# Last projection's first operands made product by product and tied behind the fold copies; second norm's modulation sums moved ahead of the output products

## The chip, the cores and the metric

One core of a Trainium2 chip runs the whole program. The metric is device time in microseconds (us), the median over several executions. The trace quoted here is of one further execution that was profiled.

## The reference, cut to what matters

Two layers of a hybrid backbone over 1024 tokens of 1024 features, in float32, batch 1. The even layer has a convolution branch and a recurrent branch behind one input projection, each with a gate, and one output projection. The odd layer pools, gates and projects again.

```python
shift, scale, gate = split(silu(c) @ mod_w[l] + mod_b[l], 3)   # modulation, per layer
hx = rmsnorm(x, norm_g[l]) * (1 + scale) + shift
# even layer (l = 0)
va, vg, ga, xb, gb = split(hx @ ev_w_in, 5)
y_a = conformer_conv(va, vg) * silu(ga)
y_b = rglru(xb) * silu(gb)
x = x + gate * (concat(y_a, y_b) @ ev_w_out)
# odd layer (l = 1)
u, g = split(hx @ od_w_in, 2)
d = multiscale_pool(u)                       # linear along the tokens
y = einsum("bngi,gij->bngj", d, w_grp) * od_scale
x = x + gate * ((y * silu(g)) @ od_w_out)
return rmsnorm(x, final_g)
```

The kernel uses that pooling is linear: it multiplies the group matrix w_grp into the input weights of u first (the *folds*), and pools after that.

## The kernel before, in words

**Products.** Features lie on the 128 partitions, tokens along the free axis, cut into two halves of 512. Every float32 operand is split into a high part (a cast on ACT, line 98) and a low part (source minus high on DVE or POOL, line 99), and each 128x512 product is three matmuls: high by high, high by low, low by high. Large projections run as `quad`: a 2x2 blocked product done with seven block products in place of eight, on PSUM tiles `qa_`, `qc_` and `qb_`. Its right-hand operands are named b11, t1, t2, b21, t3, b22, t4 in the order in which the products use them, each with parts `h` and `l`. The seven left-hand operands (`wq_..._1` to `wq_..._7`) are made of two raw weight tiles by `wquad_steps`: sums on DVE (lines 1120 to 1129), casts on ACT, low parts on DVE. The first three products are number 1 (into `qa`), number 5 (into `qc`) and, after `qa` has been copied to `qb` on ACT (line 1156), number 6 (into `qb`). A result leaves PSUM by `put`; for the first output projection this is `x <- qc, m, x` on DVE (line 1445), that is x plus gate times product.

**Order.** The code is written in one order for all engines; a scheduler then places each engine's instructions by readiness and priority, and evictions (`tc.high_priority(offset=EVAC)`) carry a higher priority. `tc.issue_after(i)` makes what stands under it wait in this order until instruction `i` has been placed, on whatever engine.

**Stages around the change** (times of the profiled execution).

- Up to about 666 us: the last products of the convolution gate (`ga`), each multiplied into the branch `u` on DVE (line 1402), from which the operands `ya_b11` to `ya_t4` of the output projection are made.
- 666 to 749 us: the first output projection `woa`, four quads for output rows (0,1), (2,3), (4,5), (6,7). The updated stream x1 is squared and summed on the way (`n1acc`).
- Modulation of the second norm: `mod_halves` is a generator of 16 steps, eight for each half of the features. At the start of a half it loads that half of c into the one tile `cH` (line 248) and applies Silu on ACT (line 249). Each step loads two 128x512 tiles of the transposed modulation weights (`mod`, line 1357, out of a ring of four scratch tiles `t` that others use too), and DVE multiplies each by c and sums along the row (line 1358); in the second half tiny operations (128x1) finish the shift `m1` and the scale `a1` (lines 1361 and 244).

```python
for _ in range((4, 3, 0, 0)[i]): next(mods)        # gate loop, i = 0..3
for _ in range((4, 5, 0, 0)[m // 2]): next(mods)   # inside the output quad of rows m, m+1
```

- 749 to 795 us: the folds of groups 2 and 3. `fold_in` loads the group matrix (`graw`, line 258) and splits it to `gh` and `gl`; `w_raw` loads a tile of u's weights (`wr_wu`, line 1468) and splits it to `wh_wu` and `wl_wu`, the low part on POOL. Each product `fold` is copied out by ACT (`fo <- fold`, line 275) and stored by a DMA on ACT's queue (line 276), since the last projection loads its weights from there. Between them the second norm's root: row sums on PE, `rt_n <- ms_n` on ACT (line 1519), reciprocal and split on DVE (`hl_n`, line 1523), and `rs` on PE, which spreads it over the partitions. Then `scaled` (DVE, line 1563) multiplies x1 by norm and scale, in place.
- From 795 us: the last layer's input projection, quads `_v` (pooled part) and `_g` (gate) in turn. Its operands are `x_b11` and so on, split by `split_x` with the shift added (ACT line 1557, DVE line 1558).

```python
wv0 = v_weights(0, ring_first)
for i in range(KH):                      # KH = 4
    b11, b21 = x1[i][:, HALF[0]], scaled(0, KH + i)
    split_x("b21", i, b21, shift(KH + i), None)
    b12, b22 = scaled(1, i), scaled(1, KH + i)
    t = block_sums(b11, b12, b21, b22, ttile(f"xt3_{i}"), nc.vector)
    split_x("t1", i, t["t1"], None, nc.vector)
    ...                                  # then t2, t3, b22, t4 of the same i
```

Of the kernel before, what the change touches and what calls it, by code (L numbers as in the profile page):

```python
# [1 line left out]

# [1 line left out]

# [17 lines left out]
H = 512  # L22
HALF = (slice(0, H), slice(H, S))
# [28 lines left out]
def body(ctx, tc, xT, ctxT, cc, ccol, modT, modW, win, gw, wout, wu, grp, wg, wo1, small, edge, ident, outT):  # L52
# [24 lines left out]
    def ttile(name):  # L77
        return tpool.tile([P, H], F32, tag="t", name=name)
# [18 lines left out]
    def split(src, hi, lo, eng):  # L97
        return (nc.scalar.copy(hi, src),  # L98
                eng.tensor_tensor(out=lo, in0=src, in1=hi.bitcast(F32), op=sub))
# [149 lines left out]
        nc.scalar.activation(t, t, AF.Silu)  # L249


    graws = {}

    def fold_in(g, g_tile, raw_tile):
        gh, gl = [], []
# [9 lines left out]
    def fold_steps(g, kp, gs, w, out_tile):  # L265
        (gh, gl), (wh, wl) = gs, w
        for s in range(2):
            ps = psum(f"fold_{g}_{kp}_{s}")
            for i in range(4):
                kc = slice(i * 2 * P + s * P, i * 2 * P + (s + 1) * P)  # L270
                yield ps, wh[:, kc], gh[i], i == 0, False
                yield ps, wh[:, kc], gl[i], False, False
                yield ps, wl[:, kc], gh[i], False, i == 3
            o = out_tile(f"fo_{g}_{kp}_{s}")
            nc.scalar.copy(o, ps)
# [807 lines left out]
        return split(src, hi[i], lo[i], nc.vector)  # L1083


    def block_sums(b11, b12, b21, b22, t3, eng):
        eng.tensor_tensor(out=t3, in0=b22, in1=b12, op=sub)
        eng.tensor_tensor(out=b12, in0=b12, in1=b11, op=sub)
        eng.tensor_tensor(out=b11, in0=b22, in1=b12, op=sub)
        eng.tensor_tensor(out=b21, in0=b21, in1=b11, op=sub)  # L1090
        return dict(t2=b11, t1=b12, t3=t3, t4=b21, b22=b22)

    loaded, parted = [None], []


    def wquad(*args):
        ops = {}
        for _ in wquad_steps(ops, *args):
            pass
        return tuple(ops[n] for n in range(1, 8))  # L1100

    def wquad_steps(ops, src, name, ring, late=False):
        raw = []
        for i in range(2):
            r = wpool.tile([P, D], F32, tag="wr", name=f"wr_{name}_{i}")
            loaded[0] = nc.sync.dma_start(r, src[i])
            raw.append(r)
        a11, a12 = [raw[0][:, h] for h in HALF]
        a21, a22 = [raw[1][:, h] for h in HALF]

        def op(v, i):
            t = ring(f"wq_{name}_{i}")
            parted[:] = split(v, t[:, HALF[0]], t[:, HALF[1]], nc.vector)
            return t

        ops[1] = op(a11, 1)
        if late:
            ops[4] = op(a22, 4)
        s3 = ttile(f"ws_{name}")
        nc.vector.tensor_tensor(out=s3, in0=a11, in1=a21, op=sub)  # L1120
        nc.vector.tensor_tensor(out=a21, in0=a21, in1=a22, op=add)
        nc.vector.tensor_tensor(out=a11, in0=a21, in1=a11, op=sub)
        if not late:
            ops[5] = op(a21, 5)
            yield
        ops[6] = op(a11, 6)
# [261 lines left out]
    for i in range(KH):  # L1388
        (b11, b12), (b21, b22) = [[us[j][:, h] for h in HALF] for j in (i, KH + i)]
        t1, t2, t3, t4 = b11, ttile(f"yat2_{i}"), b12, b21  # L1390
        for j in (i, KH + i):
            if i:
                w = wload(win[2 * KT + j], f"ga{j}", nc.gpsimd)
            if j == KT - 1:
                next(wo_steps)
            for h in range(2):
                if i:
                    ps = psum(f"ga{j}_{h}")
                    mm3(ps, w, (hh, hl), HALF[h])
# [12 lines left out]
        for name, v in zip(BOPS[4:], (t3, b22, t4)):  # L1412
            kept[name].append(v)
        for _ in range((4, 3, 0, 0)[i]):
            next(mods)

    all_of(wo_steps)
# [128 lines left out]
    def v_weights(m, ring):  # L1546
        return wquad([wfold[(m + i) // 4][(m + i) % 4].rearrange("p k c -> p (k c)") for i in range(2)], f"v{m}", ring)


    bx = {}  # L1550
# [10 lines left out]
    def scaled(h, k):  # L1561
        v = x1[k][:, HALF[h]]
        nc.vector.scalar_tensor_tensor(out=v, in0=v, scalar=a1[:, 0, k : k + 1], in1=rs[h], op0=mult, op1=mult)
        return v

    def shift(k):
        return m1[:, 0, k : k + 1]
# [10 lines left out]
            w3.append(w_raw(3, kp, dtile)[1])  # L1578
    for kp in range(2, 4):
        fold_run(3, kp, g3, w3[kp])  # L1580
    wv0 = v_weights(0, ring_first)
    for i in range(KH):
        b11, b21 = x1[i][:, HALF[0]], scaled(0, KH + i)
        split_x("b21", i, b21, shift(KH + i), None)
        b12, b22 = scaled(1, i), scaled(1, KH + i)
        t = block_sums(b11, b12, b21, b22, ttile(f"xt3_{i}"), nc.vector)
        split_x("t1", i, t["t1"], None, nc.vector)
        split_x("t2", i, t["t2"], shift(KH + i), None)
        split_x("t3", i, t["t3"], dsh[:, i : i + 1], None)
        split_x("b22", i, b22, shift(KH + i), None)  # L1590
        split_x("t4", i, t["t4"], None, nc.vector)


    fin = [None, None]
# [528 lines left out]
```

## Time and profile before

| | before |
|---|---|
| median of three executions | 1278.54 us (1276.4 to 1279.71) |
| profiled execution | 1277.14 us, span 1275.4 us, mean granted clock 0.995 |
| PE busy | 1254.0 us, 98% |
| DVE busy | 1138.0 us, 89% |
| ACT busy | 653.7 us, 51% |
| POOL busy | 301.9 us, 24% |

The profiled execution is 1.74 us longer than its span. In the views, `out<-in` names the tiles of an instruction, `x4` counts instructions in a row of the same kind, and `[2.45 <-DVE wq_woa L99]` says that the engine had been idle for 2.45 us and what released it. A line begins with the start in us and the busy time in us. In the table of waits the three numbers are the sum, the count and the longest single wait, in us. In the table of stretches the columns are the length, then busy time and count of PE, PEld (weight loads), DVE, ACT and POOL, the granted clock, the DMA share and the GB/s.

### The profile page before, as it was taken

The page shows a single profiled execution, that of the slowest core. Times are in us where ns is not written, and L with a number is a line of the kernel's source. Part 1 is how long each engine was busy: PE and PEld are TensorE (multiplying, and loading weights), DVE is VectorE, ACT ScalarE, POOL GpSimd, SP SyncE. Part 2 cuts the span into 40 slices and gives each one's busy share as a digit, 9 for nine tenths or more (in the row PEclk, how much of TensorE's full clock was granted, in tenths as well). Part 3 has the DMA queues.
Part 4 walks back from the last instruction along what each step waited for, and adds up shares of the span by engine and source line. Part 5 has one row for each costly group of instructions (what it writes and reads, how often), then busy time and mean ns, then how long its engine had stood idle before and what let it go on. Part 6 is the DMA issues. An engine that isn't in the chain of part 4 may idle for free.

```text
span 1275.4 us, 16197 instructions
## 1 busy us (share of the span) xinstructions
PE 1254.0 (98%) x5858; PEld 1035.6 (81%) x5858; DVE 1138.0 (89%) x1745; ACT 653.7 (51%) x955; POOL 301.9 (24%) x179
## 2 busy tenths in 40 slices
PE   9999999999999999999999999999999999999996
PEld 7788888888888888888887777788888888878885
DVE  7799999999999999989969968998999987987876
ACT  8464566566656433247444446644343444644642
POOL 0015364536454467433200043000000000000003
PEclk9999999999999999999999999999999999999998
DMA  9970111111211234432418565334324334768723
GB/s 378 385 254 24 58 59 66 42 58 58 67 57 58 84 115 149 155 117 84 164 50 289 190 198 167 108 124 157 107 108 140 116 124 132 275 231 291 276 67 132
DMA packets 78705, 182.29 MB, mean 143 GB/s; under 512 B 7712, under 2 KB 23328, under 8 KB 78624
## 3 DMA queue, kind: packets, MB, share of 16 engines
q1 hardware_dynamic: 69632, 176.53, 40.5%
q10 hardware_dynamic: 8992, 4.72, 1.3%
q8 instruction: 46, 0.75, 0.2%
q14 instruction: 35, 0.29, 0.1%
HBM read 137.18 MB, written 44.04 MB: 142 GB/s over the span
## 4 chain that ended last, share of the span: by engine, by line
PE 68%; DVE 18%; DMA 7%; ACT 2%; POOL 2%; issue 2%; SPq 0%; POOLq 0%; ACTq 0%; DVEq 0%
PE wob L661 7%; PE va L661 5%; DVE conv L661 5%; PE xb L661 4%; PE vg L661 4%; DVE l L661 3%; PE g L661 3%; PE ga L154 2%; PE ga L661 2%; PE ga L153 2%; PE gb L661 2%; PE ga L155 2%; PE qb_v L1142 2%; PE qb_v L1143 2%; PE qb_g L1142 2%
## 5 line engine op out<-in xcount | busy, mean ns | idle before, releaser
L661 DVE SCALAR_TENSOR_TENSOR conv<-u,sm,conv 128x505 f32<-128x505 f32 (+6 forms) x224 | 153.7, 744 | 1.0
L1855 POOL TENSOR_TENSOR o<-x,rr 128x256 f32<-128x256 f32 (+1 forms) x10 | 9.7, 1003 | 440.7 <-ACT rr L1855 438.0
L661 ACT ACTIVATE l<-g,sm 128x512 f32<-128x512 f32 (+1 forms) x96 | 58.6, 618 | 57.7 <-PE g L661 57.0
L661 POOL TENSOR_TENSOR l<-l,l 128x1280 f32<-128x1280 f32 x16 | 47.1, 2966 | 25.6 <-ACT l L661 15.1
L661 PE MATMUL gb<-h0h,wl_gb 128*128 128x512 f32 x128 | 49.9, 390 | 0.6 <-POOL wl_gb L661 0.6
L98 ACT CAST wq_g<-wr_g 128x512 fp32r<-128x512 f32 x48 | 28.3, 621 | 42.5 <-DMA wr_g<-wg 17.0
L661 PE MATMUL va<-h0h,wl_va 128*128 128x512 f32 x128 | 49.9, 390 | 0.2 <-DVE wl_va L661 0.2
L661 PE MATMUL gb<-h0h,wh_gb 128*128 128x512 f32 x128 | 49.8, 389 | 0.0
L661 PE MATMUL gb<-h0l,wh_gb 128*128 128x512 f32 x128 | 49.8, 389 | 0.0
L661 PE MATMUL va<-h0l,wh_va 128*128 128x512 f32 x128 | 49.8, 389 | 0.0
L661 PE MATMUL va<-h0h,wh_va 128*128 128x512 f32 x128 | 49.8, 389 | 0.0
L661 PE MATMUL wob<-ybh,wh_wob 128*128 128x512 f32 x128 | 49.8, 389 | 0.0
L661 PE MATMUL wob<-ybl,wh_wob 128*128 128x512 f32 x128 | 49.8, 389 | 0.0
L661 PE MATMUL wob<-ybh,wl_wob 128*128 128x512 f32 x128 | 49.8, 389 | 0.0
L661 DVE TENSOR_TENSOR_SCAN l<-l,l 128x256 f32<-128x256 f32 (+1 forms) x32 | 48.7, 1521 | 1.1
L98 ACT CAST wq_v<-wr_v 128x512 fp32r<-128x512 f32 x48 | 28.1, 620 | 39.9 <-DMA wr_v<-wfold 22.5
L661 DVE SCALAR_TENSOR_TENSOR conv<-cL,wsum,conv 128x506 f32<-128x506 f32 (+3 forms) x70 | 48.1, 743 | 0.2
L661 POOL TENSOR_TENSOR l<-l,uc 128x1280 f32<-128x1280 f32 x16 | 47.6, 2999 | 0.0
L98 ACT CAST wq_wo<-wr_wo 128x512 fp32r<-128x512 f32 x48 | 28.7, 619 | 32.1 <-DMA wr_wo<-wo 16.4
L661 POOL TENSOR_TENSOR wl_xb<-wr_xb,wh_xb 128x1024 fp32r<-128x1024 f32 x7 | 16.8, 2405 | 114.4 <-ACT wh_xb L661 114.4
L661 PE MATMUL xb<-h0l,wh_xb 128*128 128x512 f32 x112 | 43.8, 391 | 0.0
L661 PE MATMUL xb<-h0h,wh_xb 128*128 128x512 f32 x112 | 43.8, 391 | 0.0
(622 smaller groups left out, 4372.3 us busy)
## 6 DMA issues: line engine op xcount, KB each, us to landing
modw<-modW SPq DMA_DIRECT2D x16, 512.0 KB, 10.2
x_part<-xp SPq DMA_DIRECT2D x32, 256.0 KB, 2.5
mod<-modT SPq DMA_DIRECT2D x32, 256.0 KB, 4.0
wr_v<-wfold SPq DMA_DIRECT2D x16, 512.0 KB, 4.0
wr_g<-wg SPq DMA_DIRECT2D x16, 512.0 KB, 4.7
wr_wo<-wo SPq DMA_DIRECT2D x16, 512.0 KB, 4.6
mod<-modT SPq DMA_DIRECT2D x14, 512.0 KB, 4.9
yr_t<-y_t SPq DMA_DIRECT2D x14, 512.0 KB, 6.1
```

The source lines that it names most:

```text
L98: return (nc.scalar.copy(hi, src), eng.tensor_tensor(out=lo, in0=src, in1=hi.bitcast(F32), op=sub))
L153: mm(ps, hi[:, kc], xh[k][:, cols], start=(k == 0), stop=False)
L154: mm(ps, hi[:, kc], xl[k][:, cols], start=False, stop=False)
L155: mm(ps, lo[:, kc], xh[k][:, cols], start=False, stop=(k == ks - 1))
L661: last[eng] = f(*args, **kw)
L1142: nc.tensor.matmul(ps, hi, xl[k], start=False, stop=False, skip_group_check=not first)
L1143: mm = nc.tensor.matmul(ps, lo, xh[k], start=False, stop=(k == KH - 1), skip_group_check=not first)
L1855: tail[eng] = f(*args, **kw)
```

## The change

It does four things.

1. All 16 modulation steps but two run in the gate loop: (4, 3, 6, 1) steps after its four turns where it was (4, 3, 0, 0), and (2, 0, 0, 0) inside the output quads where it was (4, 5, 0, 0).
2. The low parts of the first two tiles of u's weights in group 2 (`wl_wu_2_0` and `_2_1`) are made on DVE in place of POOL.
3. Before the last projection, all inputs of the block sums are scaled and the sums taken for every `i` first; DVE's work on the first weights `wq_v0` comes behind those sums in the order (`hold`).
4. The operands are split product by product: t1 for all `i`; then t2, b21, t3 and b22, tied in the order behind the third last, second last, last and last of the fold copies; the subtraction that makes t4 behind b21's split; t4 at the end. Two of the four `xt3` tiles come from another pool.

```diff
-            nc.scalar.copy(o, ps)
+            folded.append(nc.scalar.copy(o, ps))
...
-    def block_sums(b11, b12, b21, b22, t3, eng):
+    def block_sums(b11, b12, b21, b22, t3, eng, whole=True):
...
-        eng.tensor_tensor(out=b11, in0=b22, in1=b12, op=sub)
-        eng.tensor_tensor(out=b21, in0=b21, in1=b11, op=sub)
-        return dict(t2=b11, t1=b12, t3=t3, t4=b21, b22=b22)
+        subbed[0] = eng.tensor_tensor(out=b11, in0=b22, in1=b12, op=sub)
+        if whole:
+            eng.tensor_tensor(out=b21, in0=b21, in1=b11, op=sub)
+        return dict(t2=b11, t1=b12, t3=t3, t4=b21, b21=b21, b22=b22)
...
-            parted[:] = split(v, t[:, HALF[0]], t[:, HALF[1]], nc.vector)
+            with tc.issue_after(hold.ins) if hold else nullcontext():
+                parted[:] = split(v, t[:, HALF[0]], t[:, HALF[1]], nc.vector)
...
-        nc.vector.tensor_tensor(out=s3, in0=a11, in1=a21, op=sub)
+        with tc.issue_after(hold.ins) if hold else nullcontext():
+            nc.vector.tensor_tensor(out=s3, in0=a11, in1=a21, op=sub)
...
-        for _ in range((4, 3, 0, 0)[i]):
+        for _ in range((4, 3, 6, 1)[i]):
             next(mods)
...
-        split(raw, hi, lo, nc.gpsimd)
+        split(raw, hi, lo, nc.vector if (g, kp) < (2, 2) else nc.gpsimd)
...
-        for _ in range((4, 5, 0, 0)[m // 2]):
+        for _ in range((2, 0, 0, 0)[m // 2]):
             next(mods)
...
-    wv0 = v_weights(0, ring_first)
+    xt = [(atile if i < 2 else ttile)(f"xt3_{i}")[:, :H] for i in range(KH)]
+    xs = [block_sums(x1[i][:, HALF[0]], scaled(1, i), scaled(0, KH + i), scaled(1, KH + i), xt[i], nc.vector, False)
+          for i in range(KH)]
+    wv0 = v_weights(0, ring_first, hold=subbed[0])
     for i in range(KH):
-        b11, b21 = x1[i][:, HALF[0]], scaled(0, KH + i)
-        split_x("b21", i, b21, shift(KH + i), None)
-        ...
+        split_x("t1", i, xs[i]["t1"], None, nc.vector)
+    for name, ahead in (("t2", -3), ("b21", -2), ("t3", -1), ("b22", -1)):
+        with tc.issue_after(folded[ahead].ins):
+            for i in range(KH):
+                split_x(name, i, xs[i][name], dsh[:, i : i + 1] if name == "t3" else shift(KH + i), None)
+                if name == "b21":
+                    t4 = xs[i]["b21"]
+                    nc.vector.tensor_tensor(out=t4, in0=t4, in1=xs[i]["t2"], op=sub)
+    for i in range(KH):
+        split_x("t4", i, xs[i]["b21"], None, nc.vector)
```

What stands on the engines in consequence is shown at three places. In the names, the numbers before the last underscore are the indices in the code (`mod1_0_1` is feature tile 0, half 1), the last number is a running one.

First place: DVE after the low part of `ya_t2`, at the end of the gate loop (`ga3` is a gate product, `ws_woa0`, `wr_woa0` and `wq_woa0` are the sums, raw tiles and operands of the first output quad). Before:

```order
L99 TENSOR_TENSOR ya_t2l1_5130<-yat2_2_5325,ya_t2h1_5128 128x512
L1402 TENSOR_TENSOR u3_2067<-u3_2067,ga3_0_5465 128x512
L1120 TENSOR_TENSOR ws_woa0_5537<-wr_woa0_0_5530,wr_woa0_1_5532 128x512
L1121 TENSOR_TENSOR wr_woa0_1_5532<-wr_woa0_1_5532 128x512
L99 TENSOR_TENSOR ya_b11l1_5122<-u3_2067,ya_b11h1_5120 128x512
L99 TENSOR_TENSOR wq_woa0_1_5534<-wr_woa0_0_5530,wq_woa0_1_5534 128x512
```

Now:

```order
L99 TENSOR_TENSOR ya_t2l1_5130<-yat2_2_5325,ya_t2h1_5128 128x512
L1361 SCALAR_TENSOR_TENSOR mod1_7_0_5458,m1p_3843<-mod1_7_0_5458,cH_3844 128x512
L1361 SCALAR_TENSOR_TENSOR mod1_15_0_5461,m1p_3843<-mod1_15_0_5461,cH_3844 128x512
L1405 TENSOR_TENSOR u3_2067<-u3_2067,ga3_0_5518 128x512
L99 TENSOR_TENSOR ya_b11l1_5122<-u3_2067,ya_b11h1_5120 128x512
L1361 SCALAR_TENSOR_TENSOR mod1_0_1_5466,m1p_3843<-mod1_0_1_5466,cH_3844 128x512
L1361 SCALAR_TENSOR_TENSOR mod1_8_1_5470,m1p_3843<-mod1_8_1_5470,cH_3844 128x512
L1361 SCALAR_TENSOR_TENSOR mod1_1_1_5475,m1p_3843<-mod1_1_1_5475,cH_3844 128x512
```

The last two sums of the first half and the first sums of the second half now stand ahead of the weights of the first output quad.

Second place: DVE around the first eviction of the output projection (`x1_1<-qc_woa0`). Before:

```order
L99 TENSOR_TENSOR ya_b22l1_5636<-u6_3069,ya_b22h1_5634 128x512
L1358 SCALAR_TENSOR_TENSOR mod1_7_0_5751,m1p_3843<-mod1_7_0_5751,cH_3844 128x512
L99 TENSOR_TENSOR ya_b22l1_5636<-u7_3402,ya_b22h1_5634 128x512
L1121 TENSOR_TENSOR wr_woa2_1_5723<-wr_woa2_1_5723 128x512
L1445 SCALAR_TENSOR_TENSOR x1_1_5660<-qc_woa0_5662,m0_132,x1_1_5660 128x512
```

Now:

```order
L99 TENSOR_TENSOR ya_b22l1_5698<-u7_3402,ya_b22h1_5696 128x512
L99 TENSOR_TENSOR wq_woa0_3_5677<-wr_woa0_0_5583,wq_woa0_3_5677 128x512
L99 TENSOR_TENSOR ya_t4l0_5709<-u4_2402,ya_t4h0_5707 128x512
L99 TENSOR_TENSOR ya_t4l0_5709<-u5_2735,ya_t4h0_5707 128x512
L99 TENSOR_TENSOR ya_t4l1_5710<-u6_3069,ya_t4h1_5708 128x512
L1448 SCALAR_TENSOR_TENSOR x1_1_5722<-qc_woa0_5724,m0_132,x1_1_5722 128x512
```

The eviction is the 35th instruction behind the low part of `ya_t2` before; now it is the 64th, of which 12 behind `ya_b11l1` are modulation sums of the second half.

Third place: ACT at the last fold copies (`fo_3_3_0`, `fo_3_3_1`; the lines 1557 and 1560 are the high parts of the last projection's operands). Before:

```order
L275 COPY fo_3_3_0_6675<-fold_3_3_0_6662 128x512
L1557 ACTIVATE x_t3h1_6595<-xt3_2_6769,dsh_6319 128x512
L1557 ACTIVATE x_t3h1_6595<-xt3_3_6789,dsh_6319 128x512
L276 DMA wfold3_84<-fo_3_3_0_6675 128x4x128
L275 COPY fo_3_3_1_6691<-fold_3_3_1_6678 128x512
L1557 ACTIVATE x_b22h1_6599<-x1_7_6177,m1_134 128x512
...
L1156 COPY qb_v0_6818<-qa_v0_6816 128x512
```

Now:

```order
L1560 ACTIVATE x_b21h0_6582<-x1_5_6028,m1_134 128x512
L276 DMA wfold3_84<-fo_3_3_0_6675 128x4x128
L275 COPY fo_3_3_1_6691<-fold_3_3_1_6678 128x512
L1560 ACTIVATE x_t3h0_6594<-xt3_0_6694,dsh_6319 128x512
L1560 ACTIVATE x_t3h0_6594<-xt3_1_6695,dsh_6319 128x512
L1560 ACTIVATE x_b21h1_6583<-x1_6_6176,m1_134 128x512
...
L1159 COPY qb_v0_6818<-qa_v0_6816 128x512
```

The high parts of t3 stand behind the last fold copy now, and none of b22's stands ahead of it.

More of the change, by code (lines that the diff above doesn't have):

```diff
@@ L1 @@
-from contextlib import ExitStack
+from contextlib import ExitStack, nullcontext
 import numpy as np
@@ L249, in load_c @@
         nc.scalar.activation(t, t, AF.Silu)
-    graws = {}
+    graws, folded = {}, []
     def fold_in(g, g_tile, raw_tile):
@@ L1083, in split_op, with wquad, wquad_steps @@
         return split(src, hi[i], lo[i], nc.vector)
-    def block_sums(b11, b12, b21, b22, t3, eng):
+    def block_sums(b11, b12, b21, b22, t3, eng, whole=True):
         eng.tensor_tensor(out=t3, in0=b22, in1=b12, op=sub)
         eng.tensor_tensor(out=b12, in0=b12, in1=b11, op=sub)
-        eng.tensor_tensor(out=b11, in0=b22, in1=b12, op=sub)
-        eng.tensor_tensor(out=b21, in0=b21, in1=b11, op=sub)
-        return dict(t2=b11, t1=b12, t3=t3, t4=b21, b22=b22)
-    loaded, parted = [None], []
-    def wquad(*args):
+        subbed[0] = eng.tensor_tensor(out=b11, in0=b22, in1=b12, op=sub)
+        if whole:
+            eng.tensor_tensor(out=b21, in0=b21, in1=b11, op=sub)
+        return dict(t2=b11, t1=b12, t3=t3, t4=b21, b21=b21, b22=b22)
+    loaded, parted, subbed = [None], [], [None]
+    def wquad(*args, **kw):
         ops = {}
-        for _ in wquad_steps(ops, *args):
+        for _ in wquad_steps(ops, *args, **kw):
             pass
         return tuple(ops[n] for n in range(1, 8))
-    def wquad_steps(ops, src, name, ring, late=False):
+    def wquad_steps(ops, src, name, ring, late=False, hold=None):
         raw = []
@@ L1544, in ring_first, with v_weights @@
         return dtile(name, F32R) if tag is None else wpool.tile([P, D], F32R, tag=tag, name=name)
-    def v_weights(m, ring):
-        return wquad([wfold[(m + i) // 4][(m + i) % 4].rearrange("p k c -> p (k c)") for i in range(2)], f"v{m}", ring)
+    def v_weights(m, ring, **kw):
+        return wquad([wfold[(m + i) // 4][(m + i) % 4].rearrange("p k c -> p (k c)") for i in range(2)], f"v{m}", ring, **kw)
     bx = {}
@@ L1580, in body @@
         fold_run(3, kp, g3, w3[kp])
-    wv0 = v_weights(0, ring_first)
+    xt = [(atile if i < 2 else ttile)(f"xt3_{i}")[:, :H] for i in range(KH)]
+    xs = [block_sums(x1[i][:, HALF[0]], scaled(1, i), scaled(0, KH + i), scaled(1, KH + i), xt[i], nc.vector, False)
+          for i in range(KH)]
+    wv0 = v_weights(0, ring_first, hold=subbed[0])
     for i in range(KH):
-        b11, b21 = x1[i][:, HALF[0]], scaled(0, KH + i)
-        split_x("b21", i, b21, shift(KH + i), None)
[L1585 to L1591, printed above, removed]
+        split_x("t1", i, xs[i]["t1"], None, nc.vector)
[8 more added lines that the diff above has]
+        split_x("t4", i, xs[i]["b21"], None, nc.vector)
     fin = [None, None]
```

## The prediction

> **What bounds the kernel now.** I read the page first, then the waits of TensorE around the change, then stretches of time, and last the timelines of the engines that end those waits. The page's first part:
>
> ```profile
> PE 1254.0 (98%) x5858; PEld 1035.6 (81%) x5858; DVE 1138.0 (89%) x1745; ACT 653.7 (51%) x955; POOL 301.9 (24%) x179
> ```
>
> PE is busy for 1254.0 of 1275.4 us, so an edit that adds or removes no matmul can give back only PE's waits and slow restarts. The table of PE's waits from 590 to 830 us (sum, count, longest) lists what can be got here:
>
> ```profile
> PE qc_v L1140 <- ACT fo L275: 2.5, 1, 2.5
> PE qc_woa L1143 <- DVE wq_woa L99: 2.5, 1, 2.5
> PE qb_woa L1140 <- DVE x L1445: 1.4, 2, 0.9
> PE qc_woa L1140 <- DVE x L1445: 0.8, 1, 0.8
> PE qb_v L1142 <- DVE x_t2l L1558: 0.3, 1, 0.3
> PE qa_v L1140 <- ACT fo L275: 0.3, 1, 0.3
> ```
>
> Those are 7.8 us. Where they lie, in PE's timeline:
>
> ```profile
> 669.64 0.39 PE L1143 MATMUL qc_woa<-ya_t1h,wq_woa 128*128 128x512 f32 x1
> 678.79 0.50 PE L1140 MATMUL qc_woa<-ya_b22h,wq_woa 128*128 128x512 f32 x1 [0.83 <-DVE x L1445]
> 709.08 0.50 PE L1143 MATMUL qc_woa<-ya_t1h,wq_woa 128*128 128x512 f32 x1 [2.45 <-DVE wq_woa L99]
> 709.42 0.40 PE L1140 MATMUL qc_woa<-ya_t1h,wq_woa 128*128 128x512 f32 x1
> 709.65 0.40 PE L1142 MATMUL qc_woa<-ya_t1l,wq_woa 128*128 128x512 f32 x1
> 742.04 0.50 PE L1140 MATMUL qb_woa<-ya_t3h,wq_woa 128*128 128x512 f32 x1 [0.46 <-DVE x L1445]
> 745.99 0.47 PE L1140 MATMUL qb_woa<-ya_t4h,wq_woa 128*128 128x512 f32 x1 [0.94 <-DVE x L1445]
> 800.35 0.59 PE L1140 MATMUL qc_v<-x_t1h,wq_v 128*128 128x512 f32 x1 [2.46 <-ACT fo L275]
> 803.73 0.54 PE L1143 MATMUL qc_v<-x_t1h,wq_v 128*128 128x512 f32 x1
> 804.11 0.39 PE L1140 MATMUL qc_v<-x_t1h,wq_v 128*128 128x512 f32 x1
> ```
>
> From 709.42 to 709.65 the matmuls start 0.23 us apart, the usual pace. From 800.35 to 804.11 lie nine starts in 3.76 us (0.42 apart); at 0.23 they would take 2.05. So the wait at 800.35 cost 2.46 and then 1.7 for a slow restart, while the equally long one at 709.08 cost nothing more. How busy DVE is where these waits lie (length; then busy time and count of PE, PEld, DVE, ACT, POOL; granted clock, DMA share, GB/s):
>
> ```profile
> 666.46:678.80 12.34, 11.51 (x52) 9.21 (x50) 11.66 (x21) 10.24 (x19) 0.00 (x0) 1.00 0.68 206
> 678.80:709.10 30.30, 27.80 (x121) 22.38 (x121) 26.18 (x60) 9.75 (x17) 0.00 (x0) 1.00 0.80 284
> 794.80:830.09 35.29, 32.43 (x133) 25.80 (x133) 34.07 (x58) 23.25 (x41) 0.94 (x8) 0.95 0.33 105
> ```
>
> While the first output quad begins, DVE is busy for 11.66 of 12.34 us. Work put ahead of that quad on DVE finds almost no free time; work taken out of 678.80 to 709.10 relieves a DVE that is 86% busy. That is the whole question.
>
> **The change part by part. Added: modulation ahead of the output quad (A1, A2).** The rows for DVE's prices:
>
> ```profile
> 649.91 0.68 DVE L99 TENSOR_TENSOR ya_t2l<-yat,ya_t2h 128x512 fp32r<-128x512 f32 x1
> 678.66 2.48 DVE L99 TENSOR_TENSOR ya_t4l<-u,ya_t4h 128x512 fp32r<-128x512 f32 x4
> 681.06 0.74 DVE L1445 SCALAR_TENSOR_TENSOR x<-qb_woa,m,x 128x512 f32<-128x512 f32 x1
> 692.81 0.63 ACT L249 ACTIVATE cH<-cH 128x512 f32<-128x512 f32 x1 [3.34 <-DMA cH<-cc]
> 693.48 0.69 DVE L1358 SCALAR_TENSOR_TENSOR mod<-mod,cH 128x512 f32<-128x512 f32 x1 [2.62 <-ACT cH L249]
> 694.71 0.69 DVE L1358 SCALAR_TENSOR_TENSOR mod<-mod,cH 128x512 f32<-128x512 f32 x1
> 695.93 0.35 DVE L1361 SCALAR_TENSOR_TENSOR m<-m1p,sm 128x1 f32<-128x1 f32 x2
> 696.20 0.75 DVE L1445 SCALAR_TENSOR_TENSOR x<-qb_woa,m,x 128x512 f32<-128x512 f32 x1
> ```
>
> Start to start, a 512-element operation costs 0.60 (four from 678.66 to 681.06), a modulation sum 0.61 (two from 693.48 to 694.71, one unshown between them), a tiny one 0.135 (two from 695.93 to 696.20), an eviction 0.74. DVE's order is the same in both kernels up to the low part of ya_t2 at 649.91, which ends near 650.5. Then the changed kernel has the last two sums of the first half: 651.7. The second half of c goes into the same tile `cH`, so its load starts only then. The answer on tile `cH` gives the time from issue to landing (min, median, max):
>
> ```profile
> DMA to landing us min/median/max: 3.2/4.3/5.5
> ```
>
> With 3.2 and Silu's 0.63 the first sum of the second half, two instructions further on, starts near 656.0; DVE alone would have been there near 653. This I take as the start, and walk DVE's order from it:
>
> - To the low part of `wq_woa0_5`: 10 sums (6.1), 15 tiny ones (2.0), 12 others (7.2): 671.3. PE wants it at 669.64. **A1 = +1.7.**
> - To the low part of the last `ya_t2`: 12 sums (7.3), 15 tiny ones (2.0), 20 others (12.0): 677.3. Its last quarter is wanted 22 matmuls after that start, at 671.3 + 22x0.23 = 676.4. +0.9.
> - To the end of the first eviction: 12 sums (7.3), 17 tiny (2.3), 32 others (19.2), eviction 0.74: 685.5. PE resumes there, against 678.79 before: 6.7 later in all, so **A2, with the +0.9, = +5.0**. The wait itself is about 4.8 (0.83 of it was there before).
>
> Bounds for A1 + A2: with the landing at its maximum of 5.5 it is 9.0; with DVE not waiting for c at all, 3.7. I take 6.7, since 3.2 is a load without a queue and the operands that the other steps need are by then long made.
>
> **Added: a slow restart after that wait (A3).** Rows disagree: 1.7 after 2.46 at 800.35, 0 after 2.45 at 709.08. A wait of 4.8 is longer than both, so I take +1.7, bounds 0 and 1.7. The Trainium skill, TensorE: Matmul & The Clock Gate, Part 1, states that TensorE falls to half rate after about 3.4 us idle and regains full rate after about 3.4 us busy. By that rule A3 is sure; the slow stretch from 800.35 to 803.73, 3.4 us long, agrees with the second half of the rule, but it followed a wait of 2.46, shorter than the first half says, and there the row decides.
>
> **Added: the root behind a cast (A4).**
>
> ```profile
> 738.27 2.50 POOL L99 TENSOR_TENSOR wl_wu<-wr_wu,wh_wu 128x1024 fp32r<-128x1024 f32 x1 [14.18 <-ACT wh_wu L98]
> 755.71 1.05 ACT L98 CAST gh<-graw 128x1024 fp32r<-128x1024 f32 x1 [0.46 <-DMA graw<-grp]
> 757.14 0.48 ACT L1519 ACTIVATE rt_n<-ms_n,eps_r 128x256 f32<-128x256 f32 x1
> 757.28 4.08 DMA graw<-grp
> 759.80 0.42 DVE L1523 TENSOR_TENSOR hl_n<-rt_n,hl_n 128x256 fp32r<-128x256 f32 x1
> 760.53 1.13 PE L661 MATMUL rs<-hl_n,sel 128*128 128x256 f32 x8
> ```
>
> On ACT the cast of the second group tile (`gh_3_1`) and a fold copy now stand ahead of the root `rt_n`; before, that cast came after it. Its tile lands at 757.28 + 4.08 = 761.36. With the cast (1.05) and a copy (about 0.5) the root would start at 762.9, 5.8 later, if nothing else moved; PE has only 0.3 of slack (hl_n ends at 760.2, rs starts at 760.53). But PE arrives there 6.7 + 1.7 - 2.9 = 5.5 later itself. If the load stays where it was, PE waits 0.3; if it moves with PE, less one low part on POOL (2.50) that no longer stands ahead of it, 3.3. **A4 = +1.8**, the middle.
>
> **Added: two low parts on DVE, and the splits (A5).** DVE takes 2x1.23 (the `gl` rows of the same shape have it) where it is no longer waited for after the modulation left. In the last projection ACT's copy `qb_v<-qa_v`, which opens the third product, comes behind the high parts of t3:
>
> ```profile
> 733.94 1.23 DVE L99 TENSOR_TENSOR gl<-graw,gh 128x1024 fp32r<-128x1024 f32 x1
> 803.75 0.59 ACT L1156 COPY qb_v<-qa_v 128x512 f32<-128x512 f32 x1
> ```
>
> It ended at 804.3, just ahead of PE's third product. Four high parts at about 0.6 instead of three lie between it and the last fold copy: bounds 0 and +2.5. I take 0, since product by product t1 and t2 are early.
>
> **Removed.** R1: the wait at 709.08, **-2.45**: DVE loses 14 of the 18 sums that lay in the quads, 8.5 us, most of them ahead of it. R2: at 742.04, **-0.46**; n1acc stretched beside POOL's low part and need not now:
>
> ```profile
> 738.44 2.88 DVE L1435 TENSOR_TENSOR n1acc<-n1acc,n1q 128x512 f32<-128x512 f32 x1
> 741.91 0.68 DVE L1435 TENSOR_TENSOR n1acc<-n1acc,n1q 128x512 f32<-128x512 f32 x1
> ```
>
> Beside POOL's 2.50 at 738.27 it took 2.88, alone 0.68. (The Trainium skill, SBUF: State Buffer, "SBUF: two separate sides", calls this an exclusive lock held for the whole instruction; the rows agree, and by it the 0.94 at 745.99 stays, as POOL still makes the third and fourth.) R3: the last fold copies now have fewer splits ahead of them: 2.46 + 0.28 + 0.34 and the slow restart 1.72, **-4.80**.
>
> **Sum:** 6.7 + 1.7 + 1.8 - 2.45 - 0.46 - 4.80 = +2.5. On the profiled execution (1277.14) that is 1279.6; the median (1278.54) is 1.4 higher, so I forecast **1281.0**.
>
> **The rivals.**
>
> *Faster.* DVE catches up: in 666 to 679 operands are early, no wait exceeds 2.5, so only half of A1 + A2 (3.35) and no slow restart, A4 at 0.3: 3.65 - 7.71 = -4.1, 1274.4. For it: the 709.08 wait had no slow restart. Against it: 11.66 of 12.34 busy.
>
> *Slower, the ring of four.* The modulation loads in the gate loop cannot run ahead by more than four tiles. The answer on tile `mod`, 600 to 640 us:
>
> ```profile
> DMA to landing us min/median/max: 2.5/3.4/4.8
> ```
>
> A turn of four tiles is worth about 3.4 us of DVE work; when loads take longer, DVE waits for each turn. Beside the heavy DMA (206 GB/s at 666) the load can take 5.5, as c's did; two turns then add 2x(5.5 - 3.4) = 4.2 to A2. 1285.2. It decides if loads take over 3.4 us there.
>
> *Slower, the last projection.* A5 at its upper bound, +2.5, with a restart of 1.7: also +4.2, 1285.2. For it: ACT has four more high parts tied behind fold copies; against it: most stand behind the copies.
>
> **How the numbers follow.** Forecast 0.47, faster 0.18, ring of four 0.20, last projection 0.15. About 0.3% (3.8 us) is what a measurement of this kernel can tell from no change. The forecast (+2.5) lies within it; the rivals at -4.1 and +6.7 lie outside. So faster 0.18, same 0.47, slower 0.35. Range: from the faster rival, 1274.4, to the slower ones, 1285.2 and 1.5 more for A4's upper end (3.3 for 1.8), 1286.7. The forecast's own range is 1278.0 to 1283.3 (A1 + A2 3.7 to 9.0).
>
> **What would show each step.** A1, A2: two waits in the first output quad, on `wq_woa` and, near 5 us, on `x` by its first eviction; DVE over 95% busy from 656 to 685. A3: starts 0.42 apart after it. A4: `rs` waiting for `hl_n` for 1 to 2 us, ACT idle on `graw` ahead of it. R1, R3: no wait over 0.5 in the second quad, nor at `qc_v` and `qb_v`. The forecast is wrong if the first quad's waits stay under 3 us (faster), or if DVE waits for `mod` or PE for `x_t2`, `x_b21` (slower).

## The result, and the profile after

| | before | changed |
|---|---|---|
| median of 20 executions | 1279.38 us | 1285.78 us |
| lowest and highest | 1275.21, 1286.35 | 1279.42, 1290.77 |
| profiled execution | 1277.14 us (span 1275.4, clock 0.995) | 1288.09 us (span 1286.3, clock 0.991) |

The ratio is 1.0046 (95% interval 1.003 to 1.0061), that is 3.8 to 7.8 us slower: inside the range, but not the likeliest case. The two profiled executions lie 10.95 us apart, since the one of before is 2.2 us under its median and the other 2.3 us over. So the stages below add up to more than the medians differ by (6.4).

The waits of TensorE in the changed kernel, from 590 to 840 us (sum, count, longest):

```profile
PE qc_woa L1143 <- DVE x L1448: 4.1, 1, 4.1
PE rs L661 <- POOL wl_wu L99: 3.4, 1, 3.4
PE qc_woa L1146 <- DVE wq_woa L99: 1.3, 1, 1.3
PE qb_woa L1143 <- DVE x L1448: 0.8, 1, 0.8
PE qc_woa L1143 <- ACT wq_woa L98: 0.6, 1, 0.6
```

The waits at 709 us (`wq_woa` in the second quad), at `qa_v`, `qc_v` and `qb_v` are gone, and one of the two in the last output quad; waits of 0.6 and 1.3 at the start of the first quad, one of 4.1 by the first eviction and one of 3.4 at `rs` have come.

To see where the time lies, I cut the program at TensorE's first matmul of five tiles. The timeline of before:

```profile
666.46 0.39 PE L1140 MATMUL qa_woa<-ya_b11h,wq_woa 128*128 128x512 f32 x1
754.33 0.64 PE L661 MATMUL ms_n<-n1acc,ones 128*32 128x128 f32 x16
794.86 0.50 PE L1140 MATMUL qa_v<-x_b11h,wq_v 128*128 128x512 f32 x1 [0.28 <-ACT fo L275]
1102.09 0.39 PE L1140 MATMUL qa_wo<-y_b11h,wq_wo 128*128 128x512 f32 x1
1210.05 0.39 PE L1143 MATMUL qa_wo<-y_b21h,wq_wo 128*128 128x512 f32 x1
```

and of the changed kernel:

```profile
667.81 0.39 PE L1143 MATMUL qa_woa<-ya_b11h,wq_woa 128*128 128x512 f32 x1
760.80 0.43 PE L661 MATMUL ms_n<-n1acc,ones 128*32 128x128 f32 x8
806.90 0.39 PE L1143 MATMUL qa_v<-x_b11h,wq_v 128*128 128x512 f32 x1
1109.80 0.39 PE L1143 MATMUL qa_wo<-y_b11h,wq_wo 128*128 128x512 f32 x1
1221.49 0.39 PE L1146 MATMUL qa_wo<-y_b21h,wq_wo 128*128 128x512 f32 x1
```

The last row of each is the start of the last piece of the `qa_wo` products. The differences of neighbouring rows give four stages: **A** output quads (`qa_woa` to `ms_n`: 87.87 before, 92.99 now), **B** root and folds (`ms_n` to `qa_v`: 40.53, 46.10), **C** input projection (`qa_v` to `qa_wo`: 307.23, 302.90), **D** last output projection (107.96, 111.69). The same for every run that follows, as the difference to before, from one profiled execution each; the ratio is that of all its executions to those of before beside it (one slow execution of before, 4496.81 us, is left out):

| kernel | A | B | C | D | ratio (95%) |
|---|---|---|---|---|---|
| changed | +5.1 | +5.6 | -4.3 | +3.7 | 1.0046 (1.003 to 1.0061) |
| changed again | +5.1 | +5.5 | -4.5 | +2.8 | 1.0044 (1.0028 to 1.0061) |
| sums back | -2.4 | -0.7 | +1.3 | +2.6 | 1.0015 (1.0002 to 1.0028) |
| sums only | +5.8 | +0.2 | -1.8 | -0.1 | 1.0035 (1.0022 to 1.0049) |
| root first | +5.6 | -0.7 | -2.0 | +2.5 | 1.0034 (1.0022 to 1.0046) |
| projection only | +2.1 | -0.7 | +0.9 | +2.4 | 1.0016 (1.0004 to 1.0028) |
| ties earlier | +0.2 | -0.7 | -0.2 | +0.1 | 0.9987 (0.9971 to 1.0002) |
| c early | +3.6 | +5.7 | -4.0 | +4.4 | 1.0043 (1.0028 to 1.0058) |
| copy first | -0.5 | -0.6 | -3.5 | +2.1 | 0.9965 (0.9951 to 0.998) |
| lows on POOL | +7.7 | +0.4 | +2.0 | +3.3 | 1.0072 (1.0044 to 1.0099) |
| hl_n free | +6.1 | +0.5 | -3.0 | +2.0 | 1.0032 (1.0021 to 1.0044) |
| copy first, lows on DVE | +1.3 | -0.7 | -3.6 | +3.2 | 0.9952 (0.9937 to 0.9966) |
| sums later, copy first | -0.8 | -0.2 | -5.3 | +2.0 | 0.9944 (0.9927 to 0.9962) |

Stage A contains chance of about 1.7: a slow restart that comes after some short waits and not after others (the last section). A row can differ from its ratio by more: the profiled execution of *copy first, lows on DVE* was the slowest of its eleven (1277.29), so its stages add up to +0.2 where its ratio says -6.1. The stages tell where time lies; whether a version is faster is told by the ratio.

Stage A of the changed kernel, in the timelines of DVE and of PE:

```profile
658.21 0.69 DVE L1361 SCALAR_TENSOR_TENSOR mod<-mod,cH 128x512 f32<-128x512 f32 x1 [3.07 <-ACT cH L249]
686.73 0.75 DVE L1448 SCALAR_TENSOR_TENSOR x<-qc_woa,m,x 128x512 f32<-128x512 f32 x1
```

```profile
673.34 0.50 PE L1146 MATMUL qc_woa<-ya_t1h,wq_woa 128*128 128x512 f32 x1 [1.29 <-DVE wq_woa L99]
687.53 0.80 PE L1143 MATMUL qc_woa<-ya_b22h,wq_woa 128*128 128x512 f32 x1 [4.11 <-DVE x L1448]
688.12 0.63 PE L1145 MATMUL qc_woa<-ya_b22l,wq_woa 128*128 128x512 f32 x1
690.99 0.39 PE L1146 MATMUL qc_woa<-ya_b22h,wq_woa 128*128 128x512 f32 x1
```

DVE waits 3.07 for c, and reaches the eviction 28.5 us after its first sum of the second half (658.21 to 686.73). PE resumes 19.7 after its start of the quad, 12.3 before: 7.4 later. From 687.53 eight starts take 3.46 us where 1.8 would do.

Stage B, on ACT, DVE, POOL and PE:

```profile
764.23 1.05 ACT L98 CAST gh<-graw 128x1024 fp32r<-128x1024 f32 x1 [3.05 <-DMA graw<-grp]
765.18 0.58 ACT L275 COPY fo<-fold 128x512 f32<-128x512 f32 x1
765.66 0.48 ACT L1522 ACTIVATE rt_n<-ms_n,eps_r 128x256 f32<-128x256 f32 x1
767.87 2.34 POOL L99 TENSOR_TENSOR wl_wu<-wr_wu,wh_wu 128x1024 fp32r<-128x1024 f32 x1
767.96 2.40 DVE L1525 CAST hl_n<-rt_n 128x256 fp32r<-128x256 f32 x1
770.46 2.27 PE L661 MATMUL rs<-hl_n,sel 128*128 128x256 f32 x8 [3.36 <-POOL wl_wu L99]
```

The root starts behind the cast that waits for its load, as the order said; then `hl_n`'s cast, 0.32 before, takes 2.40: a low part on POOL began 0.09 earlier, and the cast ends 0.15 behind it. After the wait PE restarts slowly.

### The profile page after: what moved, and what is told of

It reads as the page before. It is cut to its first block, busy times and chain, and to the rows that moved or that the text cites. A ratio compares the mean times of both kernels' runs of the same rounds, so it can differ in the third digit from the quotient of the medians.

```text
span 1286.3 us, 16213 instructions
## 1 busy us (share of the span) xinstructions
PE 1258.0 (98%) x5858; PEld 1038.8 (81%) x5858; DVE 1139.7 (89%) x1747; ACT 654.1 (51%) x955; POOL 296.1 (23%) x177
## 4 chain that ended last, share of the span: by engine, by line
PE 66%; DVE 18%; DMA 9%; issue 2%; ACT 2%; POOL 2%; SPq 0%; POOLq 0%; ACTq 0%; DVEq 0%
PE wob L661 7%; PE va L661 5%; DVE conv L661 5%; PE xb L661 4%; PE vg L661 4%; DVE l L661 3%; PE g L661 3%; PE fold L661 3%; DMA modw<-modW 2%; PE ga L661 2%; PE qb_v L1145 2%; PE qb_v L1146 2%; PE qb_v L1143 2%; PE gb L661 2%; PE qb_g L1145 2%
## 5 line engine op out<-in xcount | busy, mean ns | idle before, releaser
L99 DVE TENSOR_TENSOR wq_wo<-wr_wo,wq_wo 128x512 fp32r<-128x512 f32 x48 | 32.4, 687 | 13.5 <-ACT wq_wo L98 13.4
L661 PE MATMUL vg<-h0l,wh_vg 128*128 128x512 f32 x112 | 43.6, 389 | 0.0
```

The source lines that it names most:

```text
L661: last[eng] = f(*args, **kw)
```

## The experiments

**Sums back.** The changed kernel, modulation steps where they were.

```diff
-        for _ in range((4, 3, 6, 1)[i]):
+        for _ in range((4, 3, 0, 0)[i]):
-        for _ in range((2, 0, 0, 0)[m // 2]):
+        for _ in range((4, 5, 0, 0)[m // 2]):
```

> The changed kernel with the modulation steps where they were before: (4, 3, 0, 0) in the gate loop and (4, 5, 0, 0) in the output quads; its other three parts stay. On ACT the root then stands ahead of the cast of gh_3_1 again. Theory (the modulation sums ahead of the output quad cost 9.0 us there and give 3.9 back, and they also bring the late root, 5.6): no wait of about 4 us in the first output quad, rs not waiting over 1 us, the waits at wq_woa (2.5) of the second quad back; 3 to 5 us faster than before, for the last projection's waits alone. Rival (the late root comes from the low parts that went to DVE, or from the group tile's load): rs still waits over 2 us and the time stays within 2 us of before.

A goes from +5.1 to -2.4, B from +5.6 to -0.7. But it is not faster than before: 1.0015. The projection's gain is not there: C is +1.3, with a wait of 2.8 at `qb_v`. The theory held for what the sums cost and fell for the projection. It missed the second quad too: the wait at `wq_woa` came back with 0.8, not 2.5; with that and the 0.46 at 742 us gone, A is under before's.

**Sums only.** The kernel before with only those two lines changed.

> The kernel before with the modulation steps alone moved, (4, 3, 6, 1) and (2, 0, 0, 0). Theory: the wait of 4 us by the first eviction with a slow restart, then the late root with its wait at rs; the last projection's waits (2.5 with a slow restart) as before; about 5 (output quads, net) + 5.6 (root) = 10 us slower than before. Rival (root late for another reason): about 5 us slower.

A is +5.8; 1.2 of it is a wait at `ms_n` for `n1acc`, which the changed kernel does not have. B is +0.2: neither the theory's price nor its place, though here too ACT has the cast ahead of the root. So the order on ACT alone does not make the root's wait. And C is -1.8 with the old projection: no wait is left at `qa_v` and `qc_v`, since PE arrives later and ACT's last fold copies are less late. As a whole it is some 4.5 us slower (1.0035), the rival's 5 and not the theory's 10.

**Root first.** The changed kernel, the second group tile's split placed behind the root.

```diff
+            with tc.issue_after(rooted[0].ins) if g == 3 and i else nullcontext():
                 split(raw, th, tl, nc.vector if g == 2 else nc.gpsimd)
...
-        nc.scalar.activation(root, ms_n, AF.Sqrt, bias=eps_r)
+        rooted[0] = nc.scalar.activation(root, ms_n, AF.Sqrt, bias=eps_r)
```

> The changed kernel with the split of the second group tile (gh_3_1) placed behind the root in the order, and nothing else. Theory: ACT starts the root 4 to 5 us earlier, rs does not wait over 1 us and there is no slow restart behind it; 4 to 5.6 us faster than the changed kernel, about 1 us slower than before. Rival (PE is only shifted, something else such as POOL's lows or the fold weights is late next): rs waits less, but a fold product waits in its place, gain under 2 us.

B falls from +5.6 to -0.7, no fold product waits in its place. But C loses 2.3 of its gain (-2.0): what B no longer covers shows there. The wait at `qb_v` is 1.5. The whole is 1.0034 against 1.0046, some 1.5 us, where 4 to 5.6 were expected; the intervals overlap.

**Projection only.** The kernel before with parts 3 and 4 of the change.

> The kernel before with the last projection's part alone: block sums first, splits product by product behind the fold copies. Theory: the waits at qa_v, qc_v and qb_v and the slow restart go and nothing takes their place: 3.5 to 4.8 us faster than before. Rival: splits behind the fold copies make a later product wait (x_b21, x_t3 or x_b22) and the gain is under 2 us.

No gain: C is +0.9 and D +2.4. PE and ACT in its timeline:

```profile
805.24 0.50 PE L1143 MATMUL qb_v<-x_t2h,wq_v 128*128 128x512 f32 x1 [2.88 <-ACT qb_v L1159]
800.44 0.57 ACT L275 COPY fo<-fold 128x512 f32<-128x512 f32 x1
802.15 1.33 ACT L1560 ACTIVATE x_b21h<-x,m 128x512 fp32r<-128x512 f32 x2
803.37 1.33 ACT L1560 ACTIVATE x_t3h<-xt,dsh 128x512 fp32r<-128x512 f32 x2
804.60 0.59 ACT L1159 COPY qb_v<-qa_v 128x512 f32<-128x512 f32 x1
```

The wait at `qc_v` (2.46 before) has become one of 2.88 at `qb_v`: ACT's copy that opens the third product stands behind the high parts of b21 and t3, 4.2 us behind the last fold copy. The prediction's second slower rival, with its price (2.5 and a restart), in the kernel without the other parts.

**Ties earlier.** Projection only, every tie one fold copy earlier.

```diff
-    for name, ahead in (("t2", -3), ("b21", -2), ("t3", -1), ("b22", -1)):
+    for name, ahead in (("t2", -4), ("b21", -3), ("t3", -2), ("b22", -1)):
```

> Projection's part alone, with each tie one fold copy earlier: t2 behind the fourth last, b21 the third last, t3 the second last, b22 the last. The order of the last output projection (qa_wo, qc_wo, qb_wo) on TensorE is then that of the kernel before, where the run with the projection's part alone had another. Theory (the other order there costs 2.4 to 3.8 us, and the copy qb_v behind the high parts of t3 and b21 costs 2.8): from the start of qa_wo to its last product as long as before (within 0.5 us); a copy that stands only behind two high parts after the last fold copy, so a wait at qb_v under 2 us; 1 to 3 us faster than the projection's part alone. Rival (the longer last stage is chance of the run, not order): still 2 us or more longer there.

D is +0.1, and PE, DVE and ACT have the order of before in that stage, instruction by instruction. In the eight profiles whose kernels have the changed order there (changed, changed again, sums back, root first, projection only, c early, lows on POOL, hl_n free), D is +2.0 to +4.4; in sums only, with before's order, -0.1. That fits the order as the cause but does not show it: *copy first* and the two versions after it have before's order too, and lose 2.0 to 3.2 there. One place where the two orders differ, DVE in the first quad of the last output projection, in the order of the changed kernel (`wq_wo0_2_5` is an operand of the second quad, `xp0_0_1` an eviction):

```
L1782 SCALAR_TENSOR_TENSOR xp0_0_1_9487<-qc_wo0_0_9367,m1_134,xp0_0_1_9487 128x512
...
L99 TENSOR_TENSOR wq_wo0_2_5_9437<-wr_wo0_2_1_9428,wq_wo0_2_5_9437 128x512
```

Before, they stood the other way round. The waits of the changed kernel from 1090 to 1235 us include some at such operands and evictions (the longest are shown); before had 0.9 and 0.2 there:

```profile
PE qc_wo L1146 <- DVE wq_wo L99: 1.1, 1, 1.1
PE qc_wo L1143 <- DVE xp L1782: 1.1, 2, 0.8
PE qc_g L1143 <- ACT s_g L1189: 0.7, 1, 0.7
PE qb_wo L1143 <- ACT b_wo L1790: 0.6, 1, 0.6
```

The expectation of a smaller wait at `qb_v` missed: it was 3.2. As a whole it is 0.9987 against 1.0016, some 3.7 us faster than projection only, and not clear of before.

**c early.** The changed kernel, c's second half in a tile of its own, loaded at the start.

```diff
+        cH2 = vtile("cH2")
...
-            load_c(0, cH, HALF[q])
+            if q == 0:
+                load_c(0, cH, HALF[0])
+                load_c(0, cH2, HALF[1])
...
-    ... in1=cH, ...
+    ... in1=(cH, cH2)[q], ...
```

> The changed kernel with the second half of c loaded into a tile of its own at the start of the modulation steps, in place of the one tile used twice. Theory: VectorE's wait of 3.07 us for c at the end of the gate stage goes, the first eviction comes 3 us earlier, TensorE waits about 1 us there in place of 4.1 and does not restart slowly: 4 to 5 us faster than the changed kernel at that point. Rival (the ring of four modulation tiles is late next): VectorE waits for the modulation loads instead and TensorE's wait stays over 3 us.

DVE waits 0.8 for `mod` in two pieces where it waited 3.07 for c, and the eviction starts 16.2 us after `qa_woa`, 18.9 in the changed kernel. PE's wait is 5.0 all the same, since it reaches that point sooner, and a new wait of 1.9 appeared in the gate stage at 608 us. No gain (1.0043): the theory was wrong on what follows, and the rival's wait of over 3 came, but not by its cause, since the modulation loads cost DVE only 0.8. c's load is 2.8 us of the delay; the rest is DVE's queue.

**Copy first.** Projection only, with t3, b22 and t4 split behind the copy (`mid`).

```diff
-    def quad(w, name, ops, put, ahead=None):
+    def quad(w, name, ops, put, ahead=None, mid=None):
...
             evac = nc.scalar.copy(b, a)
+        if mid is not None:
+            with tc.issue_after(evac.ins):
+                mid()
```

> Projection's part alone, with t3, b22 and t4 split only behind the copy qb_v<-qa_v in the order (t2 and b21 as there). The order of the last output projection on TensorE is that of the kernel before. Theory: four high parts fewer ahead of the copy (4 x 0.65 = 2.6 us), so the wait at qb_v of 2.9 us shrinks under 0.5, nothing waits at qc_v and the later products have their operands: 3 to 4.5 us faster than the kernel before. Rival: t3 or b22 is late for the fifth or sixth product and the gain is under 1.5 us.

C is -3.5: the wait at `qb_v` is 0.4, and nothing over 0.3 came beside it. 1274.15 against 1277.85 us, faster by 0.35% (0.2 to 0.49), the first version that beats before.

D is +2.1 here, though PE, DVE and ACT have before's order in that stage, and SyncE's queue has before's order of loads and stores. A weight load comes later. Before:

```profile
1163.09 0.33 SPq L1106 DMA_DIRECT2D wr_wo<-wo  x1
1168.45 0.62 ACT L98 CAST wq_wo<-wr_wo 128x512 fp32r<-128x512 f32 x1 [3.99 <-DMA wr_wo<-wo]
```

and in copy first, whose stage D starts at 1099.03:

```profile
1162.08 0.42 SPq L1107 DMA_DIRECT2D wr_wo<-wo  x1
1166.87 0.62 ACT L98 CAST wq_wo<-wr_wo 128x512 fp32r<-128x512 f32 x1 [5.19 <-DMA wr_wo<-wo]
1181.35 0.50 PE L1143 MATMUL qb_wo<-y_t4h,wq_wo 128*128 128x512 f32 x1 [1.24 <-ACT b_wo L1800]
```

The load is issued 63.1 us into the stage, 61.0 before, behind a store of the stream (`x_part`) that SyncE's queue waits for: 6.1 us, 4.8 before. ACT's cast comes 1.5 later in the stage, and so does its copy `b_wo`, for which PE then waits. In the two versions below ACT waits 5.4 and 5.7 at the same place; in the changed kernel, with its own order, the longest such wait is 6.7, where before had 4.3. So D has at least one cause beside the order. Why the store takes longer was not tried.

**Changed again.** The changed kernel word for word.

> The changed kernel again, word for word, to see how much of its profile is chance of one execution. Theory (the wait at rs depends on whether VectorE's cast of hl_n meets POOL's low part of the next weights, 2.40 us there instead of 0.32): first eviction's wait again 4 to 5 us with a slow restart; rs waits less than 3.4 us, unless the cast is stretched again. Rival (the root is late by order, always): rs waits 3 us or more again.

B is +5.5 again: not chance. POOL and DVE in it:

```profile
766.30 2.35 POOL L99 TENSOR_TENSOR wl_wu<-wr_wu,wh_wu 128x1024 fp32r<-128x1024 f32 x1 [0.44 <-ACT wh_wu L98]
766.40 2.52 DVE L1526 TENSOR_TENSOR hl_n<-rt_n,hl_n 128x256 fp32r<-128x256 f32 x1
768.98 1.86 PE L661 MATMUL rs<-hl_n,sel 128*128 128x256 f32 x7 [2.16 <-DVE hl_n L1526]
```

Here the low part of `hl_n` meets POOL, not its cast; the price is the same.

**Lows on POOL.** The changed kernel, part 2 undone.

```diff
-        split(raw, hi, lo, nc.vector if (g, kp) < (2, 2) else nc.gpsimd)
+        split(raw, hi, lo, nc.gpsimd)
```

> The changed kernel with the low parts of wl_wu_2_0 and _2_1 on POOL again; the modulation steps and the last projection as changed. The group tile's cast then still stands ahead of the root on ACT, but the fold copy ahead of the cast, as in the run with the modulation moved alone. Theory (the late root costs 5.6 us only where its hl_n meets POOL's low part of wl_wu_3_0, and moving two lows off POOL brings that meeting about): hl_n's steps 0.3 to 0.4 us each, rs waits under 1 us, from the row sums ms_n to qa_v no longer than before within 1 us; 4 to 5.5 us faster than the changed kernel, 1 us slower than before or so. Rival (the root is late by the cast ahead of it, wherever the lows are): 2 us or more lost between ms_n and qa_v again.

B falls to +0.4, `hl_n`'s steps take 0.43 each: the theory's mechanism. Its time was wrong, 1.0072 and not better than the changed kernel. There is a wait at `qb_v` (2.9, with a restart), as in projection only, and one at `ms_n` on `n1acc` (1.8, beside POOL), as in sums only: in the changed kernel the longer wait at the root covers the one, and the lows on DVE remove the other.

**hl_n free.** The changed kernel; the low part of u's tile (3,0) is made on DVE behind `hl_n`.

```diff
+        with tc.issue_after(hl_n[0].ins) if (g, kp) == (3, 0) else nullcontext():
+            split(raw, hi, lo, nc.vector if (g, kp) < (2, 2) or (g, kp) == (3, 0) else nc.gpsimd)
```

> The changed kernel with one thing altered: the split of wu's tile (3,0) is placed behind hl_n in the order and its low part is made on VectorE, so POOL runs nothing beside hl_n; ACT's root stays behind the group tile's cast. Theory: hl_n's two steps take 0.3 and 0.4 us, TensorE's wait at rs falls by about 2.1 us to 1 us and the slow restart there (1.7 to 2) may go too: 2 to 4 us faster than the changed kernel. Rival (the late root alone costs it, not POOL): rs waits as long as before, gain under 1 us.

```profile
767.55 0.29 DVE L1527 CAST hl_n<-rt_n 128x256 fp32r<-128x256 f32 x1
767.88 0.43 DVE L1528 TENSOR_TENSOR hl_n<-rt_n,hl_n 128x256 fp32r<-128x256 f32 x1
```

B is +0.5 with the root as late as in the changed kernel (the reciprocal starts at 765.76; 766.17 there). So of 5.6 about 5 are the meeting of `hl_n` with POOL's low part and the restart that the longer wait brings; the late root alone costs 0.5 against before (1.2 against root first). As a whole it is 1.0032 against 1.0046, some 1.8 us, with intervals that overlap: part of the 5 goes in C (-3.0 in place of -4.3), where the copy at `qb_v` is waited for again (0.9).

**Copy first, lows on DVE** (the line of part 2 added to copy first) and **sums later, copy first**:

```diff
-        for _ in range((4, 5, 0, 0)[m // 2]):
+        for _ in range((3, 3, 3, 0)[m // 2]):
```

> The version with the copy qb_v first (modulation steps as before, late splits of t3, b22, t4) and in addition the first two lows of wu on VectorE, as in the changed kernel. Theory: n1acc is no longer stretched beside POOL in the last output quad, up to 2 us more than the copy-first version, 5 to 6 us faster than before. Rival (those lows bring hl_n beside POOL, or VectorE is short there): no faster than the copy-first version.

> The version with the copy qb_v first and the modulation steps later in place of earlier: (4, 3, 0, 0) in the gate loop as before and (3, 3, 3, 0) in the output quads where it was (4, 5, 0, 0). Theory (the wait of 2.2 to 2.5 us at wq_woa in the second quad is VectorE being behind by those sums): that wait shrinks under 1.2 us, none over 1 us appears in the third quad: 1 to 2 us faster than the copy-first version. Rival: the wait moves to the third quad or to the norm, no gain.

Both are faster than before: 1271.0 and 1271.18 against 1278.09 us, 0.48% and 0.56%. Against copy first the intervals overlap (0.9965, 0.9952, 0.9944), so a further gain is not shown. In the profile of sums later, the wait at `wq_woa` in the second quad is gone. From 590 to 840 us it has:

```profile
PE qc_woa L1143 <- DVE x L1451: 1.8, 2, 1.0
PE qb_woa L1143 <- DVE x L1451: 1.4, 1, 1.4
PE qb_woa L1143 <- ACT qb_woa L1159: 0.4, 1, 0.4
PE rs L661 <- DVE hl_n L1529: 0.3, 1, 0.3
```

But waits of 1.0 and 1.4 by evictions of the last quad came for it, and A is -0.8 against -0.5 in copy first. So moving sums behind the first output quad takes that wait away, and what it is worth in all stays open.

## Why the prediction was right or wrong

- **A1, A2 (+6.7): right.** 7.4 and, in the second profile, 6.9 (685.62 less 666.37, against 12.33 before). The walk through DVE's order held: 28.5 us from the first sum to the eviction, the 28.8 that were added up (61 instructions, so the eviction is the 66th behind the low part of `ya_t2`, not the 64th as stated ahead of the prediction). c's landing made DVE wait 3.07, as assumed. A1 was 0.63 + 1.29 = 1.9 for 1.7, but the 0.63 was a wait for ACT's cast, and the second profile has 0.15 + 1.29. The slow restart behind the 1.29 (1.7) is not in the sum and cost nothing: PE waits for an eviction that DVE reaches when it does, 4.1 us with that restart and 4.6 without it.
- **A3 (+1.7): right.** 1.6 and 2.0. The rule of the Trainium skill (TensorE: Matmul & The Clock Gate, Part 1: half rate after about 3.4 us idle) agrees for this wait; for shorter ones it does not, see below.
- **R1, R2 (-2.9): right in place, a little small.** The waits at 709 and 742 are gone, and the 0.94 at 745.99 is still there with 0.84, as the prediction said. Counted by the starts of the matmuls, at 0.227 us each, the two and the 0.1 make 3.5: a wait costs some 0.27 more than the idle time of its row, which counts from the end of the matmul before, and the first start behind it is 0.34 on in place of 0.23. In the same count the first quad loses 10.0 where it lost 1.4, so A1 to A3 make 8.6 for 8.4, and 8.6 - 3.5 is the +5.1 of A.
- **A4 (+1.8, bounds 0.3 to 3.3): the step that failed.** It was 5.6, beyond its bound. The late root was priced by its load and by PE's own shift, and that alone is the +0.5 of *hl_n free*. What it brought was not in the step: a later `hl_n` falls upon POOL's next low part. The row that had the price stood in the prediction, n1acc's 2.88 beside POOL, but was used only for what goes away. The Trainium skill (SBUF: State Buffer, "SBUF: two separate sides") states that VectorE and GpSimd take their shared ports by an exclusive lock held for the whole instruction; 2.40 and 2.52 beside 2.34 and 2.35 agree.
- **R3 and A5 (-4.8 and 0): right in place, for another reason.** C is -4.3 and -4.5. But A5's zero was owed to the late root, which gave ACT time: with B cured, or with the projection alone, `qb_v` waits 0.9 to 3.2 us. The projection alone gains nothing.
- **Not in the sum: D (+3.7, +2.8).** Nothing in the prediction looked beyond the projection. In the last output projection, 300 us on, the order changed as well, in code that the diff does not touch. That its cost is due to the order is not shown: three versions with before's order lose 2.0 to 3.2 there, each with a late weight load.

With 5.1 + 5.6 - 4.3 + 3.7 the profile gives 10.1 (the spans differ by 10.9: 1.35 were there before 667 us, and half a microsecond is won back at the end); the second one gives 8.9. The ratio gives 5.9. That the profiled executions show more than the median is not settled; that of before was one of its faster ones, and the changed kernel's, at a clock of 0.991, had three slow restarts between 667 and 807 us. Against the 10.1, the sum's +2.5 was low by A4's 3.8, by D's 3.7 and by 0.5 for C, while R1 and R2 took off 0.6 more than it said. The case that came is the slower one, by neither of its two rivals: DVE did not wait for `mod` in the changed kernel, and the copy was covered.

## What to carry to other kernels

When a change makes an engine late, look not only at who waits for it but at what the late instructions now run beside: here 0.3 us of VectorE cost 5 us of TensorE because they had moved next to a GpSimd instruction. Waits that follow one another cover each other, so a part tried alone may give nothing (projection only) and undoing the part that causes one wait may gain nothing (lows on POOL); add the stages up, not the waits. And measure the stages to the end of the program, not just where the diff is: here the last output projection lost 2 to 4 us in most versions, in some with another order of instructions and in some with the same.

## What the runs showed of the hardware

The slow restart of TensorE does not depend on the length of the wait alone. The same 1.29 us wait for `wq_woa`, in the changed kernel and in its second run:

```profile
674.02 0.63 PE L1145 MATMUL qc_woa<-ya_t1l,wq_woa 128*128 128x512 f32 x1
674.45 0.63 PE L1146 MATMUL qc_woa<-ya_t1h,wq_woa 128*128 128x512 f32 x1
```

```profile
671.43 0.50 PE L1146 MATMUL qc_woa<-ya_t1h,wq_woa 128*128 128x512 f32 x1 [1.29 <-DVE wq_woa L99]
672.00 0.40 PE L1145 MATMUL qc_woa<-ya_t1l,wq_woa 128*128 128x512 f32 x1
672.23 0.40 PE L1146 MATMUL qc_woa<-ya_t1h,wq_woa 128*128 128x512 f32 x1
```

After the one, starts are 0.43 apart; after the other, 0.23. The wait of 0.6 just ahead of the first does not explain it: in root first 0.6 and 1.29 follow each other at the same place, and the starts after them are 0.23 apart. Over all 14 profiles, between 580 and 1230 us and without the short matmuls of `rs` and `ms_n`, each of the 11 waits of 2.8 us and more was followed by a slow stretch that cost 1.4 to 2.8 us; of some 30 waits between 1.0 and 2.5 us six were (about 1.7 each), the others lost 0.1 to 0.2. Such a stretch shows in the granted clock (0.57 from 673.34 to 677.32 and 0.52 from 687.53 to 690.99 in the changed kernel), and over a whole execution the mean clock goes with the time, loosely: among the 20 executions of the changed kernel, the six at 0.991 took 1285.24 to 1290.77 us, the three at 0.994 1279.8 to 1284.7, with the rest between and across.
